# Two-layer hybrid decoder trunk: an eighth pair of row blocks in seven products, a weight sum formed later, and norm and split work placed on VectorE

## The chip, the cores and the metric

The kernel runs on one core of a Trainium2 chip. A core has five engines with instruction streams of their own: TensorE (PE in the profile, with its weight loads as PEld) multiplies matrices, VectorE (DVE) and GpSimd (POOL) work on elements, ScalarE (ACT) applies functions and copies, SyncE (SP) issues most of the DMAs. Operands lie in on-chip memory (tiles of 128 partitions), matmul results in PSUM banks of 512 fp32 columns. The metric is device time in microseconds for one execution of the program. Before the change it is 1268.55 us, the median of 3 runs (1267.92 to 1272.03).

## The reference

A residual stream x of 512 positions by 1024 channels goes through two layers. Each layer is an attention mixer and a feed-forward network (FFN), each followed by a layer norm of `ALPHA * x + sublayer(x)`. Layer 0 attends with compressed blocks, selected blocks and a sliding window; layer 1 with block-sparse attention over a key/value set that is made once from layer 0's output. Both attend to a second input `mem` too (256 positions), with key/value weights of their own per layer. What the change touches is the FFN, the norm and the second layer's memory weights:

```python
def layer_norm(x, g, b):
    xf = x.astype(jnp.float32)
    mu = xf.mean(-1, keepdims=True)
    var = jnp.square(xf - mu).mean(-1, keepdims=True)
    return ((xf - mu) * lax.rsqrt(var + LN_EPS) * g + b).astype(x.dtype)

def memory_attention(qm, mem, w_mem_kv):
    km, vm = jnp.split(mem @ w_mem_kv, 2, axis=-1)      # 256 x 1024 @ 1024 x 512
    ...                                                  # softmax(qm km^T) vm, 4 heads

def conv_ffn(x, w_in, conv_w, conv_b, w_out):            # D_FF = 2816
    a, b = jnp.split(x @ w_in, 2, axis=-1)
    a = sum(conv_w[k] * a_pad[:, k:k + S] for k in range(CONV_W)) + conv_b
    return (jax.nn.gelu(a) * b) @ w_out

# per layer
x = layer_norm(ALPHA * x + mix, ln1_g[layer], ln1_b[layer])
x = layer_norm(ALPHA * x + ffn, ln2_g[layer], ln2_b[layer])
```

All inputs and the output are fp32.

## The kernel before, in words

**Precision.** Every matmul of fp32 data runs as three (`mm3`): each operand is split into a rounded high part and the rest, and high x high, high x rest and rest x high are added in PSUM. The high part is made on ScalarE (`hi`, L228), the rest on VectorE (`lo`, L231). For weights that come from memory, `unit` loads 128 x 512 raw tiles, makes `hi` on ScalarE and the rest (L259) on the engine that `self.los` lists: VectorE in most places, GpSimd for an FFN's first four units and the second layer's memory weights, both in turn for some others.

**Tiling.** Positions are four row blocks `tb` of 128; the stream is in tiles nat_129 to nat_132, one per row block, 128 x 1024. The hidden width 2816 of the FFN is 22 blocks `f` of 128.

**FFN.** The *first pass* goes over f: two projections of 24 matmuls each, of 512 columns (`projT`), then `gate` (L706 to L712), which leaves `h[f]`, 128 x 512 positions, in on-chip memory. The product h x w_out isn't all done plainly. A pair of f blocks with the 512-position, 1024-channel output is a 2 x 2 by 2 x 2 product of sub-blocks, and `Blocks` computes it in seven products in place of eight. A product is 6 matmuls of 512 columns; a pair takes 42 in place of 48. Two of the seven (called A and B6) are done in the first pass: `prepare` (L85) loads the pair's four raw tiles, forms sums of weights and of h, splits them and keeps what later passes need; `first` (L125) runs the products. `take_first` (L133) adds them to the stream (L138, L141). The *second pass* runs B7 and C5 for all pairs (`second`, L143): each pair splits one h block and the two kept weight sums w1 = v11 + v12 and w3 = v12 + v22. `take_second` adds those. The *third pass* (`third`, L161) runs the last three products of each pair, with f blocks that are in no pair done plainly behind every second one. The last 5 (layer 0) or 6 (layer 1) f blocks are the tail: they are accumulated row block by row block, each followed by the norm of that row block. The kept sums live in tiles that are borrowed from other uses, by the tables `KEEP_W` and `KEEP_W4`.

**Inner norms.** `affine` does statistics on VectorE (L635, L636), subtracts the mean and multiplies by the gain, computes 1/sqrt in a chain of one-column VectorE steps (`rstd`, L643 to L651), and then scales and adds the bias. The columns 0 to `cut` are done on VectorE (L667 and L674, one instruction per 512 columns in L674), the rest by ScalarE and GpSimd in turn (L664 and L665, then L676 and L677). `cut` is `MID_CUT` for the twelve inner norms (after layer 0's mixer, layer 0's FFN and layer 1's mixer, four row blocks each); the final norm has a table of its own. Behind an inner norm, `to_xT` transposes the row block on TensorE (L242, tile psPT) and splits it into xh (ScalarE) and xl (VectorE).

**Other names.** The attention heads' results are added into tile o on VectorE (L394). `mix_end` multiplies o with the output weights and adds the result to the stream (L619). After the first row block of layer 0's last norm, the key/value product of the second layer's memory starts (`mem_kv`, with `self.los` set just ahead).

**Order.** Nobody writes the order of instructions by hand. A scheduler sets, ahead of the run, the order on each engine from the program's dependencies, priorities and the pools' buffers; instructions under `high_priority` (the norms) go ahead of others that are ready. On the chip each engine then runs its list in that order, so an instruction that waits holds all that are behind it on its engine.

## Time and profile before

| | |
|---|---|
| median of 3 runs | 1268.55 us |
| the profiled execution's own time | 1268.28 us |
| its span | 1266.5 us |
| mean granted TensorE clock | 0.985 |
| TensorE busy | 1215.7 us, 6316 matmuls |
| VectorE busy | 839.6 us, 1811 instructions |
| ScalarE busy | 635.9 us, 1345 instructions |
| GpSimd busy | 276.1 us, 364 instructions |
| moved by DMA | 133.29 MB |

In the trace layer 0's mixer ends in the norms at about 278 to 316 us, its FFN runs from there to about 690 us with the norms at 635 to 690, layer 1's attention goes on to about 880, its norms stand at 880 to 917, and layer 1's FFN takes the rest. A row of the trace's timeline gives start, duration, engine, line, operation, output and inputs by the program's tile names, the size and the count; in square brackets the idle time of the engine ahead of it and what ended that. A row of a group gives the count, then the busy time and the mean duration in ns, then the idle time of the engine ahead of the group's instructions. Matmuls are pipelined, so the spans of neighbours overlap and a group's mean is longer than their distance.

### The profile page before, as it was taken

What the parts mean: (1) busy time and instruction counts of PE and PEld (TensorE: products, weight loads), DVE (VectorE), ACT (ScalarE), POOL (GpSimd) and SP (SyncE); (2) the same over time, 40 slices, a digit from 0 to 9 for tenths busy, and PEclk for the clock granted to TensorE, in tenths of its full rate; (3) what the DMA queues carried; (4) which work ended last, traced back from release to release, by engine and by line L of the source; (5) the groups of instructions that cost most, each with busy time, mean ns of one, the idle gap of its engine ahead of it and who ended that gap; (6) DMA issues with size and microseconds to landing.
All of it is one profiled execution on the core that took longest, in us unless ns stands there. A gap on an engine that the chain in (4) does not pass through costs nothing.

```text
span 1266.5 us, 18512 instructions
## 1 busy us (share of the span) xinstructions
PE 1215.7 (96%) x6316; PEld 1033.3 (82%) x6316; DVE 839.6 (66%) x1811; ACT 635.9 (50%) x1345; POOL 276.1 (22%) x364
## 2 busy tenths in 40 slices
PE   7889999899999999999998999999899999999996
PEld 6878788778888888888888888887888888888885
DVE  6446897998765664467594676548976566445758
ACT  6458776673533333346444786465343434333642
POOL 0145453554000000000044434435400000000004
PEclk9889999999999999999998999999899999999998
DMA  9772110221534443315414222234144344331321
GB/s 235 214 201 73 43 43 26 76 84 34 167 116 126 140 132 103 100 64 169 134 34 117 76 83 87 72 99 118 34 151 131 119 130 137 110 93 51 130 92 67
DMA packets 168758, 133.29 MB, mean 105 GB/s; under 512 B 11191, under 2 KB 141623, under 8 KB 168664
## 3 DMA queue, kind: packets, MB, share of 16 engines
q1 hardware_dynamic: 168664, 132.11, 35.1%
q8 instruction: 50, 0.82, 0.3%
q14 instruction: 44, 0.36, 0.1%
HBM read 128.99 MB, written 3.08 MB: 104 GB/s over the span
## 4 chain that ended last, share of the span: by engine, by line
PE 81%; DVE 10%; ACT 3%; DMA 2%; issue 2%; SPq 1%; POOL 0%; DVEq 0%; ACTq 0%; POOLq 0%
PE psmm L234 40%; PE psS L234 27%; PE psPT L234 6%; PE psO L234 4%; PE psPT L242 3%; DVE pt L231 1%; DVE nat L674 1%; DVE p L409 1%; DVE st L635 1%; ACT p L414 1%; DMA kj<-in_mem_dram 1%; ACT hi L228 1%; DVE nat L667 1%; DVE nat L619 1%; DMA raw<-in_a_cmp_w_v_dram 1%
## 5 line engine op out<-in xcount | busy, mean ns | idle before, releaser
L228 ACT ACTIVATE hi<-raw 128x512 fp32r<-128x512 f32 x356 | 206.8, 623 | 276.1 <-PE psS L234 145.8
L259 DVE TENSOR_TENSOR lo<-raw,hi 128x512 fp32r<-128x512 f32 x266 | 180.8, 712 | 119.1 <-ACT hi L228 118.3
L234 PE MATMUL psmm<-xh,hi 128*128 128x512 f32 (+1 forms) x560 | 212.1, 379 | 0.0
L234 PE MATMUL psmm<-xl,hi 128*128 128x512 f32 (+1 forms) x560 | 211.8, 378 | 0.0
L234 PE MATMUL psmm<-xh,lo 128*128 128x512 f32 (+1 forms) x560 | 211.6, 378 | 0.0
L259 POOL TENSOR_TENSOR lo<-raw,hi 128x512 fp32r<-128x512 f32 x76 | 99.3, 1328 | 402.5 <-ACT hi L228 388.3
L234 PE MATMUL psS<-xh,hi 128*128 128x512 f32 (+1 forms) x408 | 152.1, 373 | 0.6 <-ACT G L883 0.6
L234 PE MATMUL psS<-xl,hi 128*128 128x512 f32 (+1 forms) x408 | 151.8, 372 | 0.0
L234 PE MATMUL psS<-xh,lo 128*128 128x512 f32 (+1 forms) x408 | 151.2, 371 | 0.0
L234 PEld LDWEIGHTS psmm<-xh,lo 128*128 128x128 f32 x560 | 105.4, 188 | 19.0
L234 PEld LDWEIGHTS psmm<-xl,hi 128*128 128x128 f32 x560 | 105.5, 188 | 18.8
L234 PEld LDWEIGHTS psmm<-xh,hi 128*128 128x128 f32 x560 | 105.3, 188 | 18.7 <-DVE qq L362 0.2
L234 PE MATMUL psmm<-hi,kj 128*128 128x512 f32 x336 | 118.4, 401 | 2.1 <-ACT kj L228 1.7
L414 ACT ACTIVATE p<-p,s 128x128 f32<-128x128 f32 (+3 forms) x144 | 80.0, 557 | 39.2 <-DVE s L409 38.6
L665 POOL TENSOR_TENSOR nat<-nat,p 128x384 f32<-128x384 f32 (+2 forms) x16 | 20.6, 1288 | 357.8 <-ACT nat L664 357.8
L418 POOL TENSOR_SCALAR p<-p,s 128x128 f32<-128x128 f32 (+3 forms) x144 | 75.7, 543 | 97.1 <-DVE s L385 49.2
L234 PEld LDWEIGHTS psS<-xh,hi 128*128 128x128 f32 x408 | 77.8, 191 | 13.7 <-ACT G L883 0.8
L234 PEld LDWEIGHTS psS<-xl,hi 128*128 128x128 f32 x408 | 77.8, 191 | 13.2 <-DVE xl L231 0.2
L234 PEld LDWEIGHTS psS<-xh,lo 128*128 128x128 f32 x408 | 77.7, 190 | 13.1
L231 DVE TENSOR_TENSOR pt<-psPT,pt 128x512 fp32r<-128x512 f32 (+2 forms) x124 | 73.5, 604 | 10.1 <-ACT pt L228 9.4
L409 DVE CUSTOM_DVE_ANT_0 p<-psS,T 128x128 f32<-128x128 f32 (+3 forms) x144 | 66.1, 483 | 19.4 <-PE psS L234 15.3
L228 ACT ACTIVATE pt<-psPT 128x512 fp32r<-128x512 f32 (+2 forms) x124 | 63.9, 530 | 25.9 <-PE psPT L242 18.1
(337 smaller groups left out, 2407.5 us busy)
## 6 DMA issues: line engine op xcount, KB each, us to landing
raw<-in_ffn_w_in_dram SPq DMA_DIRECT2D x176, 256.0 KB, 3.1
raw<-in_ffn_w_out_dram SPq DMA_DIRECT2D x116, 256.0 KB, 2.9
T<-bias_rows SPq DMA_DIRECT2D x144, 64.0 KB, 2.0
raw<-in_shared_w_kv_dram SPq DMA_DIRECT2D x24, 256.0 KB, 2.9
raw<-in_a_w_out_dram SPq DMA_DIRECT2D x16, 256.0 KB, 2.8
raw<-in_b_w_in_dram SPq DMA_DIRECT2D x16, 256.0 KB, 3.0
raw<-in_b_w_out_dram SPq DMA_DIRECT2D x16, 256.0 KB, 2.7
raw<-in_a_w_in_dram SPq DMA_DIRECT2D x14, 256.0 KB, 3.4
```

What stands on the lines that cost most here:

```text
L228: self.nc.scalar.activation(dst, src, AF.Copy)
L231: self.nc.vector.tensor_sub(dst, src, hi.bitcast(F))
L234: self.nc.tensor.matmul(o, l, r, start=start, stop=stop, skip_group_check=more)
L242: self.nc.tensor.transpose(o, i, self.ident)
L259: eng.tensor_sub(l[:, c], raw, h[:, c].bitcast(F))
L409: nc.vector.tensor_tensor_reduce(L[i], dst[i], T[:, 384 - 128 * i:512], op0=ALU.add, op1=ALU.min, scale=1.0, scalar=BIG, accum_out=nm[:, i ...
L414: nc.scalar.activation(L[i], L[i], AF.Exp, bias=nm[:, i:i + 1], scale=-1.0, accum_out=sm[:, i:i + 1])
L418: nc.gpsimd.tensor_scalar(L[i], L[i], r[:, i - qs[0]:i - qs[0] + 1], 1.0, op0=ALU.mult, op1=ALU.mult)
L619: nc.vector.scalar_tensor_tensor(self.nat[tb][:, sl], self.nat[tb][:, sl], ALPHA if first else 1.0, ps, op0=ALU.mult, op1=ALU.add)
L635: nc.vector.bn_stats(st[:, 6 * j:6 * j + 6], x[:, c0:c1])
L665: nc.gpsimd.tensor_mul(x[:, p], x[:, p], gt[:, p])
L667: nc.vector.scalar_tensor_tensor(x[:, d], x[:, d], mu, gt[:, d], op0=ALU.subtract, op1=ALU.mult)
```

## The change

Four things change.

1. `NPAIR` goes from 7 to 8: f blocks 14 and 15, which were done plainly in the third pass, form an eighth pair. Of f blocks done plainly ahead of the tail, one is left in layer 0 (three before) and none in layer 1 (two before).
2. The sum w3 = v12 + v22 is no longer made in `prepare` and kept. `second` loads v12 and v22 again, adds them on VectorE in place, and splits w3 and w1 as two halves of 512 columns in place of one of 1024. What is kept per pair is smaller (w1, w4, s4), and `keep` places it: pairs 0 to 3 in one p tile each, 4 and 5 in a kl tile and half of an ot tile, 6 in two T tiles, 7 in two pc tiles, the last two with halves of a pt tile for s4.
3. `MID_CUT` goes from 640 to 1024: the twelve inner norms run on VectorE alone, in pieces of 512 columns in both steps. ScalarE's and GpSimd's steps on columns 640 to 1024 go.
4. The rest parts of the second layer's memory weights (four units of two halves) are made on VectorE in place of GpSimd.

```diff
-NPAIR = 7
-KEEP_W = ("kj", "p", "p", "p", "p", "kl", "kl")
-KEEP_W4 = ("T", "T", "pc", "pc", "ot", "pt", "pt")
+NPAIR = 8
...
-MID_CUT = 640
+MID_CUT = 1024
...
+    def keep(self, i):
+        if i < 4:
+            x = self.t.al("p")
+            return x[:, 0:512], x[:, 512:1024], x[:, 1024:1280]
+        if i % 2 == 0:
+            self.s = self.t.al("ot" if i == 4 else "pt")
+        s = self.s[:, 256 * (i % 2):256 * (i % 2) + 256]
+        if i < 6:
+            x = self.t.al("kl")
+            return x[:, 0:512], x[:, 512:1024], s
+        tag = "T" if i == 6 else "pc"
+        return self.t.al(tag), self.t.al(tag), s
...
     def prepare(self, i):
...
-        w1, w3 = ws[:, 0:512], ws[:, 512:1024]
         wh, wl = t.al("hi", R), t.al("lo", R)
         t.hi(wh[:, 0:512], v11)
         t.lo(wl[:, 0:512], v11, wh[:, 0:512])
         nc.vector.tensor_add(w1, v11, v12)
-        nc.vector.tensor_add(w3, v12, v22)
         nc.vector.tensor_add(w4, w1, v22)
...
     def second(self, i):
         t = self.t
-        ws, h1 = self.k[i][0], self.h[2 * i]
+        w1, h1 = self.k[i][0], self.h[2 * i]
+        v12, v22 = self.raw(2 * i, 1), self.raw(2 * i + 1, 1)
         g, wh, wl = t.al("kj", R), t.al("hi", R), t.al("lo", R)
         t.hi(g[:, 0:512], h1)
         t.lo(g[:, 512:1024], h1, g[:, 0:512])
-        t.hi(wh, ws[:, 0:1024])
-        t.lo(wl, ws[:, 0:1024], wh)
+        t.nc.vector.tensor_add(v12, v12, v22)
+        for c, w in ((slice(512, 1024), v12), (slice(0, 512), w1)):
+            t.hi(wh[:, c], w)
+            t.lo(wl[:, c], w, wh[:, c])
...
         if cut:
-            nc.vector.scalar_tensor_tensor(x[:, d], x[:, d], mu, gt[:, d], op0=ALU.subtract, op1=ALU.mult)
+            for c in range(0, cut, 512):
+                c = slice(c, min(c + 512, cut))
+                nc.vector.scalar_tensor_tensor(x[:, c], x[:, c], mu, gt[:, c], op0=ALU.subtract, op1=ALU.mult)
...
-                    self.los, self.proj_tags = (nc.gpsimd,), ("mm",)
+                    self.los, self.proj_tags = (nc.vector,), ("mm",)
```

By the built programs, the change has 12 matmuls fewer (all of 512 columns), 36 loads of 256 KB more, 24 GpSimd and 24 ScalarE steps on 384 columns fewer, and on VectorE 16 sums of raw tiles and 8 rest parts of the memory weights more. Lines after the middle of the file move by 3 to 5 (L394 becomes L397, L667 becomes L672, L674 becomes L679, L259 becomes L262).

The scheduler makes a new order from it. In three places rows move that matter below. VectorE's order at the end of layer 0's mixer, in the norms of the first two row blocks (nat_129, nat_130), before; tile s is the one-column chain of `rstd`, and o_542 is where the heads' results go:

```order
L651 SCALAR_TENSOR_TENSOR s_792_3704<-s_793_3705,s_792_3704 128x1
L647 SCALAR_TENSOR_TENSOR s_801_3746<-s_800_3745,s_802_3747 128x1
L674 SCALAR_TENSOR_TENSOR nat_129<-nat_129,s_792_3704,p_3631 128x512
L674 SCALAR_TENSOR_TENSOR nat_129<-nat_129,s_792_3704,p_3631 128x128
L648 SCALAR_TENSOR_TENSOR s_801_3746<-s_801_3746 128x1
L231 TENSOR_TENSOR pt_3596<-psPT_3594,pt_3595 128x384
L649 SCALAR_TENSOR_TENSOR s_800_3745<-s_801_3746,s_800_3745 128x1
L650 SCALAR_TENSOR_TENSOR s_801_3746<-s_800_3745,s_802_3747 128x1
L651 SCALAR_TENSOR_TENSOR s_800_3745<-s_801_3746,s_800_3745 128x1
L231 TENSOR_TENSOR xl_3655<-psPT_3721,xh_3654 128x4x128
L674 SCALAR_TENSOR_TENSOR nat_130<-nat_130,s_800_3745,p_3631 128x512
L674 SCALAR_TENSOR_TENSOR nat_130<-nat_130,s_800_3745,p_3631 128x128
```

The last head's `L394 TENSOR_TENSOR o_542` follows right behind these. Now, the same place:

```order
L650 SCALAR_TENSOR_TENSOR s_799_3738<-s_798_3737,s_800_3739 128x1
L679 SCALAR_TENSOR_TENSOR nat_129<-nat_129,s_791_3701,p_3631 128x512 x2
L651 SCALAR_TENSOR_TENSOR s_799_3738<-s_799_3738 128x1
L397 TENSOR_TENSOR o_542<-psO_3517,ot_3608 64x256
L652 SCALAR_TENSOR_TENSOR s_798_3737<-s_799_3738,s_798_3737 128x1
L653 SCALAR_TENSOR_TENSOR s_799_3738<-s_798_3737,s_800_3739 128x1
L234 TENSOR_TENSOR xl_3655<-psPT_3716,xh_3654 128x4x128
L654 SCALAR_TENSOR_TENSOR s_798_3737<-s_799_3738,s_798_3737 128x1
L679 SCALAR_TENSOR_TENSOR nat_130<-nat_130,s_798_3737,p_3631 128x512 x2
```

The add into o_542 stands ahead of the rest of nat_130's norm, and behind nat_129's, in which two pieces of 512 columns stand where one of 512 and one of 128 stood.

VectorE's order at the end of layer 0's first FFN pass, before; L707, L709 and L712 are the gate of one of the last f blocks, and each lo_ row with 128x1024 is a pair's weight split of the second pass:

```order
L231 TENSOR_TENSOR lo_5981<-kj_4171,hi_5980 128x1024
L707 SCALAR_TENSOR_TENSOR qq_5881<-psS_5831,cw,qq_5881 128x511
L709 SCALAR_TENSOR_TENSOR qq_5881<-psS_5831,cw,qq_5881 128x510
L231 TENSOR_TENSOR kj_6017<-o_3896,kj_6017 128x512
L712 TENSOR_TENSOR pt_3901<-qq_5881,psmm_5832 128x512
L231 TENSOR_TENSOR lo_6000<-p_4369,hi_5999 128x1024
L231 TENSOR_TENSOR lo_6019<-p_4562,hi_6018 128x1024
L707 SCALAR_TENSOR_TENSOR qq_5957<-psS_5907,cw,qq_5957 128x511
L138 TENSOR_TENSOR qq_5967<-qq_5967,psPT_4259 128x512
```

Now, from the same gate on (its rows are L712, L714 and L717; L150 is the sum w3 in place):

```order
L150 TENSOR_TENSOR raw_6065<-raw_6065,raw_6067 128x512
L712 SCALAR_TENSOR_TENSOR qq_5889<-psS_5839,cw,qq_5889 128x511
L714 SCALAR_TENSOR_TENSOR qq_5889<-psS_5839,cw,qq_5889 128x510
L150 TENSOR_TENSOR raw_6091<-raw_6091,raw_6093 128x512
L717 TENSOR_TENSOR pt_3881<-qq_5889,psmm_5840 128x512
L234 TENSOR_TENSOR lo_6019<-raw_6013,hi_6018 128x512
L234 TENSOR_TENSOR lo_6019<-p_4346,hi_6018 128x512
L150 TENSOR_TENSOR raw_6117<-raw_6117,raw_6119 128x512
L234 TENSOR_TENSOR lo_6045<-raw_6039,hi_6044 128x512
L234 TENSOR_TENSOR lo_6045<-p_4537,hi_6044 128x512
L712 SCALAR_TENSOR_TENSOR qq_5965<-psS_5915,cw,qq_5965 128x511
L138 TENSOR_TENSOR qq_5975<-qq_5975,psPT_4236 128x512
```

Ahead of the adds of the first products (L138, L141) stand the weight splits of three pairs, as before, and the sums of six; the sums of the last two pairs stand behind the first L138 row. The split lo_6097 of the fifth pair comes some 15 rows later.

GpSimd's order in the norms after layer 0's FFN, before; raw_6706 to raw_6766 are memory weights, and L371 is a cast in the memory's keys:

```order
L665 TENSOR_TENSOR nat_131<-nat_131,p_6486 128x384
L259 TENSOR_TENSOR lo_6706<-raw_6707,hi_6705 128x512
L259 TENSOR_TENSOR lo_6706<-raw_6711,hi_6705 128x512
L371 CAST kj_6696<-kj_6696 64x256
L259 TENSOR_TENSOR lo_6751<-raw_6752,hi_6750 128x512
L259 TENSOR_TENSOR lo_6751<-raw_6756,hi_6750 128x512
L677 TENSOR_TENSOR nat_131<-nat_131,p_6487 128x384
L259 TENSOR_TENSOR lo_6761<-raw_6762,hi_6760 128x512
L371 CAST kj_6696<-kj_6696 64x256
L259 TENSOR_TENSOR lo_6761<-raw_6766,hi_6760 128x512
L259 TENSOR_TENSOR lo_7045<-raw_7046,hi_7044 128x512
L665 TENSOR_TENSOR nat_132<-nat_132,p_6486 128x384
```

Now:

```order
L262 TENSOR_TENSOR lo_7081<-raw_7082,hi_7080 128x512
L374 CAST kj_6737<-kj_6737 64x256
L262 TENSOR_TENSOR lo_7081<-raw_7086,hi_7080 128x512
L374 CAST kj_6781<-kj_6781 64x256
L374 CAST kj_6737<-kj_6737 64x256
```

The norm's rows and the memory weights' rows are gone from GpSimd; what stays are casts and the weights that were there for another use.

More of the change, by code (lines that the diff above doesn't have):

```diff
@@ L84, in prepare @@
         a, c, b, d = h1[:, 0:256], h1[:, 256:512], h2[:, 0:256], h2[:, 256:512]
-        ws = t.al(KEEP_W[i])
-        if KEEP_W[i] == "p":
-            s4 = ws[:, 1024:1280]
-        else:
-            if "s" not in self.k:
-                self.k["s"] = [t.al("kj"), 0]
-            n = self.k["s"][1]
-            s4 = self.k["s"][0][:, 256 * n:256 * n + 256]
-            self.k["s"][1] += 1
-        w4 = t.al(KEEP_W4[i])
+        w1, w4, s4 = self.keep(i)
         v11, v12, v22, v21 = self.raw(2 * i, 0), self.raw(2 * i, 1), self.raw(2 * i + 1, 1), self.raw(2 * i + 1, 0)
-        w1, w3 = ws[:, 0:512], ws[:, 512:1024]
         wh, wl = t.al("hi", R), t.al("lo", R)
@@ L114, in prepare @@
         nc.vector.tensor_add(s4, s4, b)
-        self.k[i] = ws, s4, w4
+        self.k[i] = w1, s4, w4
         return g, wh, wl
```

## Prediction

> **What bounds the kernel now.** I read the page's totals first, then the busy time by stretch, then what TensorE waits for in the three stretches that lose time, then single instructions there.
>
> ```profile
> span 1266.5 us, 18512 instructions
> PE 1215.7 (96%) x6316; PEld 1033.3 (82%) x6316; DVE 839.6 (66%) x1811; ACT 635.9 (50%) x1345; POOL 276.1 (22%) x364
> PE 81%; DVE 10%; ACT 3%; DMA 2%; issue 2%; SPq 1%; POOL 0%; DVEq 0%; ACTq 0%; POOLq 0%
> ```
>
> TensorE is busy for 96% of the span and is 81% of the chain that ended last; VectorE is 10% of it. So a microsecond of matmul is a microsecond of time almost everywhere, and the 10% has to be found. The view by stretches (its columns: stretch, length, busy time and instructions of TensorE, weight loads, VectorE, ScalarE, GpSimd, the granted TensorE clock, DMA share, GB/s) finds it:
>
> ```profile
> 315.00:554.00 239.00, 239.00 (x1088) 199.37 (x1088) 138.21 (x232) 91.47 (x156) 0.00 (x0) 1.00 0.40 119
> 278.00:315.00 37.00, 32.46 (x230) 28.91 (x231) 33.30 (x89) 16.01 (x32) 17.66 (x17) 1.00 0.16 49
> 635.00:690.00 55.00, 50.12 (x319) 45.12 (x318) 42.19 (x96) 26.09 (x52) 27.08 (x24) 0.94 0.23 68
> 880.00:917.00 37.00, 32.57 (x213) 29.16 (x213) 35.31 (x92) 15.11 (x29) 17.98 (x17) 0.91 0.11 32
> 664.00:668.00 4.00, 1.93 (x13) 1.36 (x13) 3.86 (x6) 2.44 (x5) 3.85 (x4) 1.00 0.35 111
> 668.20:674.80 6.60, 5.95 (x27) 5.72 (x28) 3.99 (x6) 2.32 (x5) 4.58 (x6) 0.50 0.54 153
> 886.00:890.00 4.00, 1.73 (x13) 1.59 (x14) 3.99 (x17) 0.95 (x3) 0.54 (x1) 1.00 0.00 0
> 890.10:896.80 6.70, 5.15 (x17) 4.09 (x16) 6.50 (x15) 2.64 (x6) 3.97 (x4) 0.50 0.01 2
> ```
>
> The first FFN pass (first row) loses nothing. The three stretches with inner norms do: A, the norm after layer 0's mixer, idles 37 - 32.46 = 4.5 us; B, after layer 0's FFN, 4.9; C, after layer 1's mixer, 4.4. B and C lose more than that: after 4 us in which TensorE was busy for under half (1.93 and 1.73), the granted clock is 0.50 for some 6.7 us. At that clock 5.95 us of matmul could have been 2.97, so the half clock costs about 3.0 in B and 5.15/2 = 2.6 in C. What is to be had from the norms is thus at most 4.5 in A, 7.9 in B and 7.0 in C. The waits of TensorE in B:
>
> ```profile
> PE psPT L242 <- DVE nat L674: 2.7, 3, 1.4
> PE psmm L234 <- DVE kj L231: 1.1, 1, 1.1
> PE psmm L234 <- POOL lo L259: 0.7, 1, 0.7
> PE psPT L242 <- POOL nat L677: 0.3, 1, 0.3
> ```
>
> They are on VectorE's last norm step (L674), with two smaller ones on GpSimd. Why VectorE is late is in its own instructions: the same instruction early in B and late in B, and what GpSimd ran in the latter time.
>
> ```profile
> 638.22 0.15 DVE L648 SCALAR_TENSOR_TENSOR s<-s 128x1 f32<-128x1 f32 x1
> 663.86 1.19 DVE L648 SCALAR_TENSOR_TENSOR s<-s 128x1 f32<-128x1 f32 x1
> 663.78 1.26 POOL L259 TENSOR_TENSOR lo<-raw,hi 128x512 fp32r<-128x512 f32 x1
> 285.85 1.01 DVE L674 SCALAR_TENSOR_TENSOR nat<-nat,s,p 128x512 f32<-128x512 f32 x2
> 665.75 2.93 DVE L674 SCALAR_TENSOR_TENSOR nat<-nat,s,p 128x512 f32<-128x512 f32 x2
> 665.59 2.95 POOL L259 TENSOR_TENSOR lo<-raw,hi 128x512 fp32r<-128x512 f32 x2
> 667.46 0.66 PE L242 MATMUL psPT<-ident,nat 128*128 128x128 f32 x4 [1.40 <-DVE nat L674]
> ```
>
> A one-column step took 1.19 us in place of 0.15, and a 1.01 us pair took 2.93, each ending with GpSimd's own subtraction beside it. Those 3.0 us stand straight ahead of the transposes for which TensorE waited 1.40 us, and just behind it the clock halves at about 668.
>
> **The change part by part.** *The eighth pair.* Four f blocks fewer are done plainly (two per layer), at 42 matmuls a pair against 48: 6 fewer per layer, 12 in all, of 512 columns.
>
> ```profile
> 361.50 5.44 PE psS L234 x24
> ```
>
> 24 of them take 5.44 us, 0.227 each, so 12 x 0.227 = **-2.7 us**. The spans of 0.38 us that the page gives for one overlap; the pitch is what counts.
>
> *The second pass.* Each pair now loads two blocks again and adds them on VectorE, and the split comes in two halves. TensorE needs 12 x 0.227 = 2.72 us a pair. VectorE's rows in this pass of before:
>
> ```profile
> 559.85 3.69 DVE L141 SCALAR_TENSOR_TENSOR nat<-nat,qq 128x512 f32<-128x512 f32 x6
> 571.99 1.22 DVE L231 TENSOR_TENSOR lo<-kl,hi 128x1024 fp32r<-128x1024 f32 x1
> 573.13 0.68 DVE L231 TENSOR_TENSOR kj<-v,kj 128x512 fp32r<-128x512 f32 x1
> 573.73 1.29 DVE L259 TENSOR_TENSOR lo<-raw,hi 128x512 fp32r<-128x512 f32 x2
> raw<-in_ffn_w_out_dram SPq DMA_DIRECT2D x116, 256.0 KB, 2.9
> ```
>
> A pair cost VectorE 1.22 + 0.68 = 1.90; now it is a sum (0.68), the split of h (0.68) and two halves (1.29): 2.65, nearly the 2.72 of TensorE. Ahead of them stand the adds of the first products, 3.69 and two of 0.68: 5.05. Had nothing been done earlier, TensorE would wait 5.05 + 8 x 2.65 - 8 x 2.72 = 4.5 us, and 2.0 more for the first pair's sum, split of h and one half, with no product to cover it: 6.5 a layer. But in the order of the changed kernel six of the eight sums and the weight halves of three pairs stand on VectorE ahead of those adds (of layer 0; layer 1's sums stand in the same way), in the first pass, where it is busy for 138 of 239 us: 6 x 0.68 + 3 x 1.29 = 7.9 us of cover against 6.5. I set lo_6097 (the fifth pair) against the products of the four before it, and there 1.2 us of slack is left. What uses that up is paid in full. The 36 more loads of 256 KB land in 2.9 us and are issued that far ahead on SP's queue, which has five raw tiles to fill. In the third pass a pair costs VectorE two splits of 0.68, half a one (0.42) and a weight's two halves (1.29), 3.1 us, under the 18 x 0.227 = 4.08 of TensorE, so that fewer plain blocks between the pairs cost nothing. I take 0.4 a layer, **+0.8 us**, with 0 and 13 as bounds.
>
> *The inner norms.* Per norm a ScalarE and a GpSimd step on 384 columns go twice, and VectorE does four pieces of 512. An undisturbed piece is 3.69/6 = 0.615, so 2.46 a norm against 1.89 before (0.88 for 640 columns of L667, and the 1.01 above):
>
> ```profile
> 635.03 0.88 DVE L667 SCALAR_TENSOR_TENSOR nat<-nat,s,p 128x640 f32<-128x640 f32 x1
> L667 DVE SCALAR_TENSOR_TENSOR nat<-nat,s,p 128x640 f32<-128x640 f32 x12 | 12.7, 1057 | 0.0
> L674 DVE SCALAR_TENSOR_TENSOR nat<-nat,s,p 128x512 f32<-128x512 f32 x15 | 13.7, 922 | 0.2
> L674 DVE SCALAR_TENSOR_TENSOR nat<-nat,s,p 128x128 f32<-128x128 f32 x12 | 7.9, 657 | 0.0
> ```
>
> The three groups' means are 1.057 + 0.922 + 0.657 = 2.64 a norm, however. If the stretch goes with GpSimd's steps, VectorE saves 0.18 a norm and its small steps run at 0.15; if not, four pieces at 0.922 cost 3.69, 1.05 more. I take the first, since the stretched rows are those with a GpSimd row beside them; the second is a rival below.
>
> *The second memory's splits* leave GpSimd for VectorE, eight halves in B:
>
> ```profile
> L259 POOL TENSOR_TENSOR lo<-raw,hi 128x512 fp32r<-128x512 f32 x12 | 16.0, 1352 | 14.2 <-ACT hi L228 12.1 <-issue 1.8
> L259 DVE TENSOR_TENSOR lo<-raw,hi 128x512 fp32r<-128x512 f32 x5 | 5.8, 1166 | 0.2 <-POOL nat L677 0.2
> ```
>
> VectorE gets 8 x 0.65 = 5.2 us more. It loses 5.8 - 5 x 0.65 = 2.5 of stretch on the five it has. Behind these eight in its queue wait the norm steps of the next row blocks, but norms have the higher priority in the scheduler.
>
> *What this gives by stage.* B: GpSimd's two waits go (1.0). The chain ahead of 667.46 is some 3.0 us shorter by the two stretched rows, less what the moved halves take of it; of its waits of 1.40 and 0.71 I count 1.0 as saved. With that TensorE is busy for about 3 of the 4 us ahead of 668, so the half clock goes, 3.0. Sum **-5.0 us**, bounds -7.9 and +1. A and C:
>
> ```profile
> PE psPT L242 <- DVE nat L674: 1.5, 3, 0.7
> PE psO L234 <- DVE pt L231: 0.8, 1, 0.8
> PE psO L234 <- DVE o L394: 0.6, 1, 0.6
> 889.63 1.69 PE L234 MATMUL psO<-pt,v 128*128 128x256 f32 x8 [1.93 <-DVE o L394]
> 892.87 0.79 PE L234 MATMUL psmm<-hi,kj 128*128 128x512 f32 x1 [1.55 <-ACT kj L228]
> ```
>
> In A 2.9 of the 4.5 idle are waits on VectorE (the first three rows); the last head's o add now stands ahead of the last norm step of the second row block, two pieces earlier. I take two thirds of 2.9: **-2.0 us**, bounds -3.5 and +1. In C one wait of 1.93 on an o add and one of 1.55 on a split stand around a half clock; I count half of the two, **-1.7 us**, and leave the half clock where it is, since about 1.3 us of idle still falls in its 4 us. Bounds: -4.3, with the 2.6 of the clock, and +1.
>
> **Sum.** The profiled execution took 1268.28 us (span 1266.5), 0.27 under the median of 1268.55. 1268.28 - 2.7 + 0.8 - 5.0 - 2.0 - 1.7 = 1257.7, and on the median's footing **1258.0 us**.
>
> [...]
>
> **The rivals.** (1) *The half clock in B stays*, because it isn't the 1.40 us wait that sets it. For it: A idles 4.5 us in 37 without any fall, so idle time alone doesn't tell. Against it: both falls come behind 4 us with under half busy. 1258.0 + 3.0 = 1261.0. [...]
>
> (2) *The norms give nothing.* VectorE's added pieces and halves use up what the stretch gave, and A, B and C stay as they are. For it: VectorE is busy for 33.3 of 37 and 35.3 of 37 us in A and C, and load moved onto a full engine rarely frees it. Against it: the busy time contains the stretch. 1268.55 - 2.7 + 0.8 = 1266.7.
>
> (3) *The second pass waits.* The sums stand early in the order, but each holds a raw tile until its split, and the five tiles also carry the last first-pass loads; if these come late, the cover goes and both layers pay 6.5. 1258.0 - 0.8 + 13.0 = 1270.2.
>
> (4) *Slower: VectorE's pieces stay stretched and its queue is the path.* Two operands in memory beside ScalarE's and the DMA's traffic stretch L674, not GpSimd. Then 12 norms cost 1.05 more each, 12.6, all in stages where VectorE sets the end, and nothing comes back: 1268.55 - 2.7 + 0.8 + 12.6 = 1279.3. It decides from 5.7 us of added path (1.9 to win back and 3.8 to tell), 0.48 a norm. Against it: the pieces of 0.615 ran just behind the first pass, where ScalarE and DMA work (91 of 239 us, 119 GB/s) and GpSimd does nothing.
>
> That the change doesn't do what it says I exclude: the new program has 12 matmuls fewer, 24 steps on 384 columns fewer on GpSimd and 36 loads more.
>
> **How the numbers follow.** Chances: forecast 0.52 (its own range 1252 to 1264), rival 1 0.18, rival 2 0.13, rival 3 0.08, rival 4 0.09. Changes under 0.3% (3.8 us, 1264.7 to 1272.4) can't be told from none. Faster: 0.52 + 0.18 + 0.04 of rival 2 = 0.74. Same: 0.09 of rival 2, 0.06 of rival 3, 0.02 of a mild rival 4 = 0.17. Slower: 0.09. The range reaches down to all stages at their ceilings but the last few tenths (1268.28 - 2.7 - 3.5 - 7.9 - 4.3 = 1249.9) and up to just above rival 2: 1250 to 1267.
>
> **What would show it.** 12 matmuls fewer and a first pass without idle: the first term. The granted clock at 1.00 through B, and no stretched L648 row beside a norm: the -5.0. Waits of TensorE on nat and o under 2 us in A and C. No wait on lo or kj between the two passes. Wrong it would be by a wait on lo in the second pass of over 1 us, by norm pieces of 0.9 us with GpSimd silent, or by a half clock in a new place.

## The result

The changed kernel takes **1259.37 us** (median of 4 runs, 1258.98 to 1259.72), the kernel before 1268.43 (median of its 4 runs by then, 1267.92 to 1272.03): a ratio of **0.9922, 95% interval 0.9904 to 0.9941**, faster by 9.1 us. The forecast was 1258.0 in 1250 to 1267.

The totals of the profiled execution after:

```profile
span 1257.4 us, 18606 instructions
PE 1210.6 (96%) x6304; PEld 1032.2 (82%) x6304; DVE 847.6 (67%) x1861; ACT 628.4 (50%) x1347; POOL 237.8 (19%) x332
```

TensorE has 12 matmuls fewer; VectorE is busy for 8 us more and GpSimd for 38 us less. Where the 9.1 us of span come from is read from one and the same instruction in both traces. The timeline of VectorE gives such marks: the first statistics step of a norm stage (L635, now L638) and a gate in the dense part of an FFN's first pass (L712, now L717). Before:

```profile
268.77 0.68 DVE L635 BATCH_NORM_STATS2 st<-nat 128x6 f32<-128x512 f32 x1
494.89 0.69 DVE L712 TENSOR_TENSOR v<-qq,psmm 128x512 f32<-128x512 f32 x1 [2.33 <-PE psmm L234]
632.22 0.69 DVE L635 BATCH_NORM_STATS2 st<-nat 128x6 f32<-128x512 f32 x1
880.83 0.69 DVE L635 BATCH_NORM_STATS2 st<-nat 128x6 f32<-128x512 f32 x1
1036.76 0.69 DVE L712 TENSOR_TENSOR v<-qq,psmm 128x512 f32<-128x512 f32 x1 [2.33 <-PE psmm L234]
```

After:

```profile
268.59 0.68 DVE L638 BATCH_NORM_STATS2 st<-nat 128x6 f32<-128x512 f32 x1
492.75 0.69 DVE L717 TENSOR_TENSOR v<-qq,psmm 128x512 f32<-128x512 f32 x1 [1.86 <-PE psmm L237]
628.73 0.69 DVE L638 BATCH_NORM_STATS2 st<-nat 128x6 f32<-128x512 f32 x1
873.97 0.69 DVE L638 BATCH_NORM_STATS2 st<-nat 128x6 f32<-128x512 f32 x1
1028.80 0.69 DVE L717 TENSOR_TENSOR v<-qq,psmm 128x512 f32<-128x512 f32 x1 [2.33 <-PE psmm L237]
```

The differences are -0.18, -2.14, -3.49, -6.86 and -7.96, and -9.1 at the end of the span (1257.4 against 1266.5). From mark to mark: stage A -2.0, the rest of layer 0's FFN -1.4, stage B with layer 1's attention -3.4, stage C -1.1, and layer 1's FFN from its first pass on -1.1. The same marks are used for every experiment below.

Stage C's mark needs care. In the changed kernel it stands 12 matmuls later in TensorE's work (8 transposes and 4 products of 256 columns, about 1.2 us at their distances of 0.10 and 0.11), because VectorE comes to this step later in a new order. So B is also cut at TensorE's first product of 512 columns in layer 1's attention, which is the end of B's norms. Shown are the stretch from B's mark to that product and the one from C's mark to the gate, first of before, then of after. Behind the length stand TensorE's busy time and, in brackets, its matmuls:

```profile
632.22:688.73 56.51, 51.63 (x325) 46.39 (x324) 43.91 (x100) 24.85 (x50) 25.81 (x23) 0.94 0.23 66
880.83:1036.76 155.93, 151.50 (x779) 129.45 (x779) 110.67 (x222) 63.14 (x113) 17.15 (x16) 0.98 0.36 109
628.73:682.54 53.81, 50.40 (x325) 46.20 (x324) 44.52 (x108) 20.58 (x42) 7.45 (x8) 0.94 0.23 69
873.97:1028.80 154.83, 149.90 (x768) 128.28 (x767) 106.64 (x217) 57.90 (x104) 8.14 (x6) 0.98 0.37 109
```

B's norms gain 2.7 us (53.81 against 56.51, with 325 matmuls in both), and layer 1's attention and stage C together 1.8.

The stretches by busy time, columns as in the prediction:

```profile
278.00:315.00 37.00, 34.00 (x248) 30.88 (x249) 32.19 (x88) 11.78 (x26) 8.46 (x9) 1.00 0.15 47
626.00:680.00 54.00, 50.59 (x317) 45.96 (x316) 44.04 (x106) 19.38 (x39) 7.45 (x8) 0.94 0.23 69
655.20:659.20 4.00, 1.99 (x17) 1.79 (x15) 4.00 (x8) 3.15 (x8) 1.38 (x1) 1.00 0.76 239
659.50:666.00 6.50, 5.39 (x25) 5.42 (x26) 6.24 (x19) 1.10 (x3) 3.24 (x6) 0.50 0.43 124
872.00:909.00 37.00, 32.07 (x208) 28.99 (x207) 35.21 (x91) 10.12 (x21) 9.40 (x8) 0.91 0.11 29
```

A is as forecast: TensorE idles 3.0 us of 37 in place of 4.5. B isn't: the half clock is still there, now from 659.4 on, and ahead of it lies a stretch of 4 us with TensorE busy for 1.99. All of TensorE's waits in B:

```profile
PE psmm L237 <- DVE kj L234: 3.4, 1, 3.4
```

and the timeline of the three engines at that time:

```profile
660.61 0.55 PE L237 MATMUL psmm<-hi,o 128*128 128x256 f32 x1 [3.42 <-DVE kj L234]
657.15 0.67 DVE L638 BATCH_NORM_STATS2 st<-nat 128x6 f32<-128x512 f32 x1
657.75 0.66 DVE L262 TENSOR_TENSOR lo<-raw,hi 128x512 fp32r<-128x512 f32 x1
658.34 1.21 DVE L653 SCALAR_TENSOR_TENSOR s<-s,s 128x1 f32<-128x1 f32 x1
659.48 0.41 DVE L234 TENSOR_TENSOR kj<-psmm,kj 64x256 fp32r<-64x256 f32 x1
660.03 0.43 DVE L234 TENSOR_TENSOR kj<-psmm,kj 64x256 fp32r<-64x256 f32 x1
657.82 1.72 POOL L262 TENSOR_TENSOR lo<-raw,hi 128x512 fp32r<-128x512 f32 x1 [357.18 <-DVE st L638]
```

The waits of before (4.8 us in all) are gone, and one of 3.4 has come. TensorE is at the value product of the second layer's memory, which needs one of two mm banks, and these come free when VectorE has split the memory's keys (kj). That split, in two halves, stands behind a statistics step, a weight split and a one-column step that takes 1.21 us, with GpSimd's first split after 357 idle us beside it.

### The profile page after: what moved, and what is told of

Its sections match the earlier page's. It is cut to its first block, busy times and chain, and to the rows that moved or that the text cites. A ratio compares the mean times of both kernels' runs of the same rounds, so it can differ in the third digit from the quotient of the medians.

```text
span 1257.4 us, 18606 instructions
## 1 busy us (share of the span) xinstructions
PE 1210.6 (96%) x6304; PEld 1032.2 (82%) x6304; DVE 847.6 (67%) x1861; ACT 628.4 (50%) x1347; POOL 237.8 (19%) x332
## 4 chain that ended last, share of the span: by engine, by line
PE 84%; DVE 7%; DMA 3%; ACT 3%; issue 1%; SPq 1%; POOL 0%; DVEq 0%; POOLq 0%; ACTq 0%
PE psmm L237 41%; PE psS L237 28%; PE psPT L237 6%; PE psO L237 4%; PE psPT L245 4%; DVE pt L234 1%; DMA kj<-in_mem_dram 1%; DVE p L412 1%; DMA raw<-in_ffn_w_out_dram 1%; DVE nat L672 1%; ACT p L417 1%; ACT kj L231 1%; DVE nat L679 1%; ACT pt L231 1%; DVE nat L622 1%
## 5 line engine op out<-in xcount | busy, mean ns | idle before, releaser
L231 ACT ACTIVATE hi<-raw 128x512 fp32r<-128x512 f32 x370 | 216.4, 624 | 286.9 <-PE psS L237 158.0
L262 DVE TENSOR_TENSOR lo<-raw,hi 128x512 fp32r<-128x512 f32 x270 | 178.8, 693 | 108.1 <-ACT hi L231 106.4
L262 POOL TENSOR_TENSOR lo<-raw,hi 128x512 fp32r<-128x512 f32 x68 | 88.8, 1328 | 438.9 <-DVE st L638 357.2
L237 PE MATMUL psmm<-hi,kj 128*128 128x512 f32 x328 | 114.3, 401 | 3.2 <-ACT kj L231 2.2
L237 PEld LDWEIGHTS psmm<-hi,kj 128*128 128x128 f32 x328 | 61.5, 189 | 16.1 <-ACT kj L231 2.6
```

Of the source, the lines that this page charges most:

```text
L231: self.nc.scalar.activation(dst, src, AF.Copy)
L237: self.nc.tensor.matmul(o, l, r, start=start, stop=stop, skip_group_check=more)
L262: eng.tensor_sub(l[:, c], raw, h[:, c].bitcast(F))
```

## The experiments

On the chips of the experiments the runs of one kernel lie up to 8 us apart (the kernel before: 1264.1 to 1272.1 over all of them), as the first 270 us move by -3.0 to +1.1 and half-clock stretches come as 3.4, 6.8 or 10.2 us. Parts of 1 to 4 us are therefore judged by the stage in which they act, from the marks of each profiled execution against the kernel before, and by the median only beside it. All in us; "start" is up to the first mark, B takes in layer 1's attention, and FFN 1 goes to the end of the span:

| kernel | median | ratio, 95% interval | start | A | FFN 0 | B | C | FFN 1 |
|---|---|---|---|---|---|---|---|---|
| the change | 1259.37 | 0.9922 [0.9904, 0.9941] | -0.2 | -2.0 | -1.4 | -3.4 | -1.1 | -1.1 |
| norms alone | 1264.85 | 0.9971 [0.9958, 0.9985] | -3.0 | -1.9 | 0.0 | -1.6 | +0.9 | 0.0 |
| memory alone | 1264.62 | 0.9968 [0.9957, 0.9978] | +1.1 | +0.8 | 0.0 | -4.0 | +0.2 | 0.0 |
| pair alone | 1263.11 | 0.9966 [0.9953, 0.9979] | +1.1 | 0.0 | -1.4 | -0.1 | -1.4 | -1.0 |
| norms and memory | 1263.40 | 0.9966 [0.9955, 0.9978] | -1.4 | -1.8 | 0.0 | -2.5 | +0.1 | +0.1 |
| GpSimd beside | 1265.21 | 0.9979 [0.9967, 0.9992] | -0.6 | +1.1 | -1.4 | -1.7 | +0.7 | -1.9 |
| ScalarE beside | 1258.70 | 0.9931 [0.9911, 0.9951] | +0.2 | -1.8 | -1.4 | -4.3 | +0.2 | -2.1 |
| values in another bank | 1253.81 | 0.9887 [0.9870, 0.9903] | +0.6 | -1.9 | -1.2 | -8.8 | -1.1 | -1.5 |
| norms only in A | 1260.91 | 0.9950 [0.9934, 0.9967] | 0.0 | -1.9 | -1.4 | -4.7 | +1.0 | -1.7 |
| before, another bank | 1265.93 | 0.9980 [0.9969, 0.9992] | +0.3 | 0.0 | 0.0 | -1.6 | +0.5 | 0.0 |
| both banks | 1259.72 | 0.9931 [0.9914, 0.9947] | -1.5 | +0.5 | -1.4 | -8.8 | +4.5 | -1.9 |
| memory back | 1261.63 | 0.9950 [0.9933, 0.9967] | 0.0 | -1.9 | -1.4 | -1.9 | -1.0 | -0.6 |
| other bank, 640 in B | 1256.22 | 0.9919 [0.9903, 0.9936] | -0.2 | -1.9 | -1.4 | -5.4 | -0.5 | -2.1 |

C's mark lies 12 matmuls later in all nine kernels with the pair edit, so their B and C can be compared among themselves, but not with the four others. The next table compares all; "attention and C" is the rest of B and C together. Each stage is from one execution, and the half clock in B is not equally long in all of them: 3.4 us of it cost up to 1.7. That is an estimate from the granted clock of 0.50; in the changed kernel's C, products of 512 columns stand 0.43 us apart at this clock and 0.23 at 1.00.

| kernel | half clock in B | B's norms | attention and C |
|---|---|---|---|
| before | 6.8 | 0 | 0 |
| the change | 6.8 | -2.7 | -1.8 |
| norms alone | 6.8 | -1.8 | +1.0 |
| memory alone | 3.4 | -4.2 | +0.4 |
| pair alone | 3.4 | +0.6 | -2.1 |
| norms and memory | 3.4 | -2.5 | +0.1 |
| GpSimd beside | 6.8 | -1.1 | +0.1 |
| ScalarE beside | 3.4 | -3.7 | -0.5 |
| norms only in A | none | -4.0 | +0.3 |
| before, another bank | 6.8 | -1.7 | +0.6 |
| memory back | 6.8 | -1.3 | -1.6 |
| other bank, 640 in B | 3.4 | -4.8 | -1.2 |

Values in another bank and both banks have no half clock in B, and their first 512-column product stands elsewhere in the order. In C the half clock is 6.8 us in all kernels but ScalarE beside (10.2) and both banks (10.2 in two stretches). A moved by +0.8 in memory alone, whose order in A is that of before; that is the scatter to reckon with.

### The parts alone

**Norms alone** on the kernel before:

```diff
-MID_CUT = 640
+MID_CUT = 1024
...
-            nc.vector.scalar_tensor_tensor(x[:, d], x[:, d], mu, gt[:, d], op0=ALU.subtract, op1=ALU.mult)
+            for c in range(0, cut, 512):
+                ...
```

> The kernel before with the inner norms wholly on VectorE (cut 1024, pieces of 512 columns) and nothing else of the change. Theory of the prediction: the stretch of VectorE's steps goes with GpSimd's norm steps, so stages A and C give their 2.0 and about 1.1 us (as the changed kernel's trace shows them) and B a part of its 3.3, since GpSimd still splits the memory weights there: 1268.4 - 2.0 - 1.1 - 1.5 = about 1264. Rival (moved work is simply added): the four pieces cost as much as what goes, 1268 to 1269. Rival (the pieces stay stretched): 12 x 1.05 more, about 1280.

A gives its -1.9 whole, B -1.6, C nothing (+0.9). Of the two sizes that the theory took from the changed kernel, A's holds; C's was the shift of the mark.

**Memory alone:**

```diff
-                    self.los, self.proj_tags = (nc.gpsimd,), ("mm",)
+                    self.los, self.proj_tags = (nc.vector,), ("mm",)
```

> The kernel before with only the second memory's weight splits on VectorE. Theory: GpSimd's eight splits of 1.35 us go from B, and with them a part of the stretch and the wait of 0.7 us; 5.2 us of VectorE work comes in their place, so about -1 us: 1267.5. Rival (the splits were what stretched VectorE most in B, 16 us of GpSimd against 10 of norm steps): B's whole 3.3 us, 1265. Rival (VectorE's queue is the path): +2 to +5 us, 1270 to 1273.

B gives -4.0, of which up to 1.7 is a half clock of 3.4 us in place of 6.8. The theory had put -1 on it; the first rival is nearer: GpSimd's eight splits held B up more than the norms' steps did, though with the half clock set aside the lead is under 1 us. 5.2 us of work more on VectorE took none of it back that shows.

**Pair alone:** `keep`, `prepare` and `second` as in the change, the cut and the memory as before:

```diff
-NPAIR = 7
+NPAIR = 8
 MID_CUT = 640
```

> The kernel before with only the eighth pair, the smaller kept tiles and the sum made in the second pass. Theory: 12 matmuls fewer give -2.7 us, and the loss of cover in layer 1's third pass, which the changed kernel's trace shows at 0.7 to 1.0, takes some back: about -1.9, 1266.5. Rival (the second pass waits for VectorE): up to 6.5 us a layer back, 1270 to 1279. Rival (nothing is lost): -2.7, 1265.7.

Layer 0 gives -1.4 (6 matmuls at 0.227 are 1.36), with no wait between the passes; layer 1's FFN -1.0. But layer 1's attention and C give -2.1 together, with no edit in them: the scheduler makes a new order there, and in the kernels with the pair edit TensorE idles 1.9 to 2.0 us between its first 512-column product and C's mark, in the others 2.9 to 3.1. The expectation had no such term. The median is 5.4 us under the 1268.56 of the kernel before beside it, below even the rival's 1265.7.

**Norms and memory** together, on the kernel before:

```diff
-MID_CUT = 640
+MID_CUT = 1024
...
-                    self.los, self.proj_tags = (nc.gpsimd,), ("mm",)
+                    self.los, self.proj_tags = (nc.vector,), ("mm",)
```

> Both edits to VectorE's load, without the eighth pair: the changed kernel with its pair part undone. Theory (the parts act in separate stages and add up): the changed kernel's 1259.4 + 1.9 = 1261.3. Rival (the eighth pair's smaller tiles also help the norm stages, or hurt them): off from 1261.3 by over 1 us.

The time is 2.1 us off the expected 1261.3, as the rival had it: the pair edit does act outside the FFNs. In B the two parts give -2.5, less than the memory's -4.0 alone, with a half clock of 3.4 us in both. So they don't add up: something that comes with the norms takes back 1.5 us. All of TensorE's waits in B are on splits of kj tiles here too, 4.1 us of them on the memory keys' ahead of the value product:

```profile
PE psmm L234 <- DVE kj L231: 4.6, 2, 4.1
```

### What stretches VectorE

Two steps on 384 columns were put back into each inner norm of the changed kernel, into a scratch tile that nobody reads, once on GpSimd and once on ScalarE. The outputs don't depend on them.

```diff
+            nc.gpsimd.tensor_tensor(z, gt[:, 640:D], mu.to_broadcast([128, 384]), op=ALU.mult)
...
             y = self.rstd(var)
+            nc.gpsimd.tensor_tensor(z, bt[:, 640:D], y.to_broadcast([128, 384]), op=ALU.mult)
```

> The changed kernel, with two GpSimd multiplications on 384 columns added to each inner norm, one that needs the mean and one that needs 1/sqrt, into a scratch tile that nobody reads. The order on the other engines stays as it is but for a few rows. Theory (GpSimd beside it is what stretches VectorE's norm steps): the norm pieces, 0.70 and 0.65 us in the changed kernel, go to 0.8 or more in the stages with norms, one-column steps of about 1 us come back, and A and B lose 1 to 3 us. Rival (ScalarE and DMA traffic stretch them): pieces as in the changed kernel, time 1259 to 1260.

```diff
+            nc.scalar.activation(z, gt[:, 640:D], AF.Identity, bias=mu)
...
             y = self.rstd(var)
+            nc.scalar.activation(z, bt[:, 640:D], AF.Copy, scale=y)
```

> The changed kernel with the same two steps added on ScalarE in place of GpSimd (384 columns, into a scratch tile that nobody reads). Theory: VectorE's norm pieces stay as in the changed kernel, within 0.03 us in the mean; ScalarE has room, so the time is 1259 to 1261. Rival (ScalarE's traffic stretches them): pieces of 0.8 us and more, and a loss of 1 to 3 us.

VectorE's norm pieces in B (groups by shape; count, busy time, mean in ns), in the changed kernel:

```profile
L672 DVE SCALAR_TENSOR_TENSOR nat<-nat,s,p 128x512 f32<-128x512 f32 x8 | 6.0, 778 | 0.0
L679 DVE SCALAR_TENSOR_TENSOR nat<-nat,s,p 128x512 f32<-128x512 f32 x8 | 5.8, 744 | 0.0
```

with GpSimd's steps beside (the same two lines, now L676 and L686):

```profile
L676 DVE SCALAR_TENSOR_TENSOR nat<-nat,s,p 128x512 f32<-128x512 f32 x8 | 6.6, 843 | 0.0
L686 DVE SCALAR_TENSOR_TENSOR nat<-nat,s,p 128x512 f32<-128x512 f32 x8 | 9.1, 1163 | 0.0
PE psmm L238 <- DVE kj L235: 4.9, 1, 4.9
```

with ScalarE's:

```profile
L676 DVE SCALAR_TENSOR_TENSOR nat<-nat,s,p 128x512 f32<-128x512 f32 x8 | 6.0, 778 | 0.0
L686 DVE SCALAR_TENSOR_TENSOR nat<-nat,s,p 128x512 f32<-128x512 f32 x8 | 5.8, 744 | 0.0
```

ScalarE's steps leave the means at 778 and 744 to the nanosecond; GpSimd's raise them to 843 and 1163, though nobody waits for them. By stage they cost 3.1 us in A (from -2.0 to +1.1), 1.7 in B and 1.8 in C, with the half clock as in the changed kernel in all three. The wait for the keys' split grows from 3.4 to 4.9. That GpSimd beside it stretches VectorE, and that this sets the time, is shown; the rival with ScalarE's traffic is out.

### Which part pays where

**Norms only in A:** the norm gets its cut from the caller.

```diff
-                self.norm_xT(tb, gt, bt)
+                self.norm_xT(tb, gt, bt, 640)
...
-            self.norm_xT(tb, *state["gb"])
+            self.norm_xT(tb, *state["gb"], 640 if l else MID_CUT)
```

> The changed kernel, with the inner norms wholly on VectorE only after layer 0's mixer; after layer 0's FFN and layer 1's mixer the cut is 640 again. The single parts gave in stage A -1.9 us from the norms, in B -4.2 from the memory part alone but -2.5 with the norms beside it, in C +0.1 to +0.9 from the norms. Theory (norms on VectorE pay in A alone): 1 to 2 us under the changed kernel, 1257.5 to 1258.5. Rival (the differences in B and C come from the phase of the half clock, not from the norms): 1259 to 1260, no difference.

A keeps its -1.9 and B is at -4.7, better than the change's -3.4, in an execution without a half clock in B. But C stands at +1.0 against -1.1, and the median isn't better (1260.91). The expected 1 to 2 us don't come. Why C is worse here than in pair alone, with the same norms in C, isn't known.

**Memory back**, on the changed kernel:

```diff
-                    self.los, self.proj_tags = (nc.vector,), ("mm",)
+                    self.los, self.proj_tags = (nc.gpsimd,), ("mm",)
```

> The changed kernel with the second memory's splits on GpSimd again: norms and pair stay. Theory (in B the memory's splits pay, -4.2 us alone, and the norms little beside them): A -1.9 as in the changed kernel, B at -1.8 as with the norms alone, 1.5 us less than in the changed kernel: about 1261. Rival (the norms pay in B, and the memory part adds nothing to them): B at -3.3 or better, 1259 to 1259.5.

As the theory has it: A -1.9, B -1.9, 1.5 less than in the change. The wait for the keys' split is there without the memory's splits on VectorE as well, so it is the norms that bring it. Norms alone has it too, with 2.62 us; memory alone, pair alone and norms only in A don't have it ahead of the value product. A shorter wait for a kj split that frees an mm bank stands ahead of other products, 1.10 in the kernel before. Memory back's waits in B:

```profile
PE psmm L237 <- DVE kj L234: 3.5, 1, 3.5
PE psPT L245 <- DVE nat L679: 1.6, 2, 1.2
```

### The new wait

The value product takes the bank of the heads' outputs, which is free at that time:

```diff
-        ps = self.pj()
+        ps = self.ps("O") if rt == "p" else self.pj()
         for b in range(2):
             for k in range(KC):
```

> The changed kernel, with the value product of the second layer's memory in the PSUM bank of the heads' outputs (free at that time) in place of one of the two mm banks. TensorE's new wait of 3.4 us in B, for the split of the memory keys that frees the mm bank, has no cause then. Theory (this wait holds up B and drops the clock): the wait falls under 1 us, no half clock between 640 and 690, B gives 3 to 6 us more: 1253.5 to 1256.5. Rival (TensorE then waits as long for the weights' splits or for the norm of the last row block, which stand on VectorE at the same time): 1258.5 to 1259.5, with a wait on lo or nat of 2 to 3 us and the half clock still there.

**1253.81 us**, ratio 0.9887 [0.9870, 0.9903], 5.6 us under the change. B goes from -3.4 to -8.8. A stretch of 55 us over B's norms now, and TensorE's only wait there:

```profile
621.00:676.00 55.00, 54.75 (x347) 48.87 (x346) 48.14 (x113) 21.67 (x44) 8.69 (x8) 1.00 0.31 93
PE psmm L237 <- ACT xh L231: 0.3, 1, 0.3
```

TensorE idles 0.25 us of 55 where it idled 4.9 in the kernel before, the one wait of 3.4 is 0.3, and the granted clock is 1.00 all through. The half clock went with the wait. VectorE is no less busy for it (48.14 of 55, against 44.04 of 54 in the changed kernel): it was the order of its work against one bank that held TensorE, not the amount.

The same edit on the kernel before:

> The kernel before, with the value product of the second layer's memory in the heads' PSUM bank, as in values_other_bank. Theory (the wait for the mm bank came with the change, which moved VectorE's work in B; before it, TensorE waited there for norm pieces and GpSimd): B moves by less than 1.5 us and keeps a half clock: 1267 to 1268.5. Rival (the bank was scarce all along, and the changed kernel's gain in B is just made larger by an edit of its own): B gives 4 to 6 us here too, 1263 to 1265.

It gives -1.6 in B, a little over the theory's bound of 1.5, and the half clock stays. Its waits are the old ones without the 1.1 on a kj split:

```profile
PE psPT L242 <- DVE nat L674: 2.3, 3, 1.4
PE psO L234 <- POOL lo L259: 0.7, 1, 0.7
PE psPT L242 <- POOL nat L677: 0.2, 1, 0.2
```

So the bank was worth 1.1 to 1.7 us before the change, and 5.4 after it.

And values in another bank with the cut back in B:

```diff
-                self.norm_xT(tb, gt, bt)
+                self.norm_xT(tb, gt, bt, 640)
```

> values_other_bank, with the norms after layer 0's FFN at the cut of 640 columns again (ScalarE and GpSimd do the rest). Theory (with the bank free, the norm pieces on VectorE are what keeps GpSimd out and B dense): GpSimd's steps bring stretch and waits on nat back, B loses 2 to 6 us against values_other_bank, 1256 to 1260. Rival (the norms never paid in B, only the memory's splits and the bank did): B within 1 us, 1253 to 1255.

With the bank free, the cut of 640 in B costs 3.4 us there (-5.4 against -8.8), of which up to 1.7 is a half clock of 3.4 us. TensorE waits 2.08 us on a norm piece again:

```profile
672.10 1.33 PE L245 MATMUL psPT<-ident,nat 128*128 128x128 f32 x5 [2.08 <-DVE nat L679]
```

So norms on VectorE do pay in B, once the wait that they bring is gone; with the bank scarce they cost there.

### Stage C

**Both banks**, on top of values in another bank:

```diff
         def head(h, g, qs, T):
-            O = self.ps("O")
+            O = self.ps("PT" if h == NH - 1 and qs[0] else "O")
```

> values_other_bank, and in the two mixers the last head's output in a PT bank, in place of the heads' single O bank, so that this head doesn't wait for the add of the one before. In VectorE's order the last o add of layer 1 then stands ahead of the second row block's first norm pieces. Theory (in C the heads' bank and the o add behind norm pieces hold TensorE, 2.7 and 2.3 us, and set the half clock): C gives 2 to 5 us more, 1249 to 1252. Rival (the split of the last head's weights pt_9505, which stands behind the same norm pieces, holds it as long): C within 1 us of values_other_bank, 1253 to 1254.5.

This is no gain but a loss: A +0.5 in place of -1.9, C +4.5 in place of -1.1, 1259.72 in all. A has a half clock of 3.4 us, which no other kernel here has, and C has 10.2 us of it in place of 6.8, so up to 1.7 us of each loss is the clock's. TensorE's rows in C, of values in another bank (first two) and of both banks:

```profile
876.62 1.84 PE L237 MATMUL psO<-pt,v 128*128 128x256 f32 x8 [2.51 <-DVE o L397]
880.50 0.80 PE L237 MATMUL psmm<-hi,kj 128*128 128x512 f32 x1 [2.04 <-ACT kj L231]
```

```profile
877.11 0.56 PE L237 MATMUL psPT<-pt,v 128*128 128x256 f32 x3 [2.08 <-DVE pt L234]
879.04 0.79 PE L237 MATMUL psmm<-hi,kj 128*128 128x512 f32 x1 [1.37 <-ACT kj L231]
893.66 1.12 PE L245 MATMUL psPT<-ident,nat 128*128 128x128 f32 x4 [3.89 <-DVE xl L234]
```

The wait for the o add turns into one of 2.08 on the split of the last head's weights, as the rival had it, and with a PT bank taken the transposes behind wait 3.89 on the split that frees another. The better version is values in another bank, without this edit.

## Why the prediction was right, and where not

**The eighth pair, -2.7.** Layer 0 gave -1.36 in the trace, the 6 x 0.227 of its matmuls. Layer 1's FFN gave between -0.6 and -2.1 in the kernels with the pair edit, -1.1 in the changed one. The distance of 0.227 was the right price in layer 0, where nothing else acts.

**The second pass, +0.8.** Too much: TensorE doesn't wait between the passes in either layer, so rival 3 is out and the early sums were cover enough. But the step that "fewer plain blocks between the pairs cost nothing" fails for layer 1, where none is left. Of the changed kernel, ScalarE and TensorE at the end of the third pass:

```profile
1212.85 1.27 ACT L231 ACTIVATE xh<-raw 128x512 fp32r<-128x512 f32 x2 [1.16 <-DMA raw<-in_ffn_w_out_dram]
1214.02 1.14 ACT L231 ACTIVATE kj<-v 128x512 fp32r<-128x512 f32 x2
1214.69 0.50 PE L237 MATMUL psPT<-hi,kj 128*128 128x512 f32 x1 [0.84 <-ACT kj L231]
```

ScalarE waits 1.16 us for a tail weight to land, and the next h split stands behind that. I had set VectorE's 3.1 against 4.08 a pair and not looked at ScalarE's in-order queue behind a DMA. In the other kernels with the pair edit this wait of TensorE is between nothing and 1.51 us, so that is the price.

**Stage A, -2.0.** Measured -2.0, and -1.8 to -1.9 in every other kernel with the norms and the heads' bank as they are; GpSimd's steps put back take 3.1. TensorE's waits on nat and o, which the forecast named, fall from 2.4 to 0.3 us between 268 and 316, while others grow by about 1. The two thirds were a guess that came out.

**Stage B, -5.0.** Measured -2.7 in its norms; with the attention it is -3.4 by the marks. The step that failed is "with that TensorE is busy for about 3 of the 4 us ahead of 668, so the half clock goes". The waits that I shortened did go, all 4.8 us of them. I hadn't asked what would be late next: the split that frees the mm bank, in VectorE's queue among the norm steps. The half clock came with it as rival 1 had it, by a wait of another place. A hint stood in my own list of waits in B, 1.1 us on a kj split, and my sum left it out. With the bank free the stage gave -8.8; wait and half clock went together there, so these runs don't price them apart. That is more than my ceiling of 7.9, which took idle time and half clock only. It left out the attention that the mark takes in, about 0.7 in the kernels with the pair edit; where the last 0.2 come from isn't shown.

Within B the forecast didn't say what the norms and what the memory's splits would give. Of the parts alone the splits gave -4.0 (-1 expected) and the norms -1.6, but 3.4 us less of half clock are in the first.

**The pieces' price.** The sum set 0.615 us, a distance between starts, against means of durations, which overlap. By durations four pieces cost 3.0 us a norm in B, against 3.3 for the three steps of before, whose 512 columns took 1.40: VectorE saves about 0.2 a norm there. But in A they cost 3.6 against 2.6, and in C 3.4 against 2.2, since the 512-column step of before took only 0.75 there. The kernel's mean of 2.64 hid this. What A gained, it gained from waits, not from cheaper steps.

**Stage C, -1.7.** C and the attention ahead of it gave -1.8, but not by the reason given; that the number fits is luck. The waits of 1.93 and 1.55 became longer, not shorter:

```profile
881.15 1.95 PE L237 MATMUL psO<-pt,v 128*128 128x256 f32 x8 [2.52 <-DVE o L397]
885.03 0.80 PE L237 MATMUL psmm<-hi,kj 128*128 128x512 f32 x1 [1.93 <-ACT kj L231]
```

Norms alone gave +1.0 in these stages. Pair alone gave -2.1 there, with the norms in C as before, so the gain came with the pair edit, by a new order of layer 1's attention that the prediction didn't foresee. Norms only in A has the pair edit too and no such gain (+0.3), so what in that order decides stays open.

**The rivals.** Rival 2 (nothing from the norms) and rival 4 (pieces stay stretched) are out by A and by GpSimd and ScalarE beside. Rival 4's sign, pieces of 0.9 us, is there in part (the first step takes 0.99 in A and 0.88 in C, but not with GpSimd silent: in A a pair of them takes 1.40 us at 302.77 and 3.40 at 297.79, with GpSimd's splits beside it), but the time came back all the same. Rival 1 happened in part. The sum came out within 1.4 us because B's miss (2.3) stood against 0.6 that the two FFNs gave beyond their -2.7 + 0.8, 0.2 of the start and a C that came out right for another reason.

## What to carry to other kernels

Before counting a removed wait as gained, write down who is next in the queue of the engine that stays busy, and which buffer or bank that instruction frees: here one bank held back 5 us of a stage whose other waits had all gone. Take a step's price from the stage it runs in, not from the kernel's mean. Work on GpSimd that nobody waits for can still cost VectorE time: here it took the mean of VectorE's last norm step in B from 744 to 1163 ns. And where runs of one kernel spread by more than a part is worth, compare the same instruction's start, stage by stage, and see that the same work lies ahead of it on the engine that counts.

## What the runs showed of the hardware

**A GpSimd step next to VectorE's two-operand steps** raised the mean of the last norm step in B (8 pieces of 512 columns) from 744 to 1163 ns, with nothing waiting for GpSimd; the same work on ScalarE left it at 744.

**The half clock** (a granted clock of 0.50) came after 4 us in which TensorE was busy for about half or less (1.99 and, in C, 1.48 of 4 in the changed kernel; 1.93 and 1.73 before; at most 2.4, in A of both banks), and not in B of values in another bank, where no wait longer than 0.3 us is left. But a low share alone doesn't bring it: in pair alone TensorE was busy for 0.98 of 3.4 us (third row below) and the clock stayed at 1.00.

```profile
877.20:881.20 4.00, 1.48 (x12) 1.26 (x10) 4.00 (x12) 0.87 (x2) 0.00 (x0) 1.00 0.00 0
881.30:887.90 6.60, 4.67 (x15) 3.90 (x16) 6.40 (x23) 1.10 (x3) 2.18 (x2) 0.50 0.01 2
664.20:667.60 3.40, 0.98 (x6) 0.78 (x6) 3.33 (x6) 2.20 (x5) 3.25 (x4) 1.00 0.33 101
```

The first two rows are C's of the changed kernel, by stretch. The half clock's stretches in the stages were 3.4, 6.8 or 10.2 us long in the profiled executions, for one and the same order of TensorE too: the changed kernel has 6.8 in B and in C, ScalarE beside 3.4 and 10.2. The falls came behind waits of different length. Those of the kernel before came behind waits of 1.40 and 1.93 us, and in B of the changed kernel the clock fell at 659.4, when the wait of 3.42 us had lasted 2.2. Only in B of GpSimd beside it fell after 3.4 us without a matmul.
